# Seven stores of a pair of feed-forward chunks, placed over two units instead of one

## The chip, the cores and the metric

The kernel runs on one core of a Trainium2 chip. A core has five engines with an instruction queue each: TensorE (PE in the profile, with its weight loads as PEld) multiplies matrices, VectorE (DVE) and ScalarE (ACT) work on tiles, GpSimd (POOL) does so more slowly, and SyncE (SP) only issues DMA transfers here. An engine takes its instructions in the order of its queue; engines wait for each other at semaphores. SBUF is the on-chip memory, PSUM the banks into which TensorE accumulates, and DRAM the memory outside the core.

The metric is the device time of one execution in microseconds, the median of the runs. The kernel before takes 2773.14 us (three runs, 2771.61 to 2774.72).

## The reference, cut to what matters

Two layers of a decoder, 1024 tokens by 1024 features, all in float32. The change is in the feed-forward half of a layer:

```python
    h2 = rmsnorm(x, norm2[l])
    up = h2 @ w_up[l]
    a, v = up[..., :D_FF], up[..., D_FF:]
    a = causal_depthwise_conv(a, conv_w[l], conv_b[l])
    x = x + (jax.nn.gelu(a, approximate=False) * v) @ w_down[l]
```

`D_FF` is 2816, so `w_up` is 1024 x 5632 and `w_down` is 2816 x 1024; the convolution looks at the present token and the two before it.

## The kernel before, in words

**Numbers in two halves.** A float32 operand goes to TensorE as a rounded part (`hi`, made by a copy on ScalarE) and the rest (`lo`, a subtraction on VectorE). `split` (L122 to L124) issues the two. Every product is then three matmuls: hi by hi, hi by lo, lo by hi.

**Seven products for eight.** Most large products are two by two block products with seven block multiplications in place of eight. That needs sums and differences of blocks: of the weights, of the activations, and of the results.

**The up projection.** The 2816 hidden features are 22 chunks `j` of 128 features. Chunks 0 and 1 are done plainly (`up_plain`, L1353). Chunks 2 to 21 are units of `up(j)` (L1394): seven products w1, w5, w6, w3, w7, w2, w4 in this order, each 12 matmuls of 128x512 through `seven` (L851), with a `yield` in the middle and one after, so that a unit has 14 steps. The results gather in PSUM banks `pa` (`u_a`), `pc` (`u_c`) and `pb` (`u_b`). Bank `pa` takes w1, then w6 on top, then w7, then w4; before each further product an engine reads what is there. L1422 and L1430 are copies on ScalarE after w1 and w6. L1439, on VectorE, adds `pa` after w7 to `u5`; then w4 is accumulated on top and read in the gating. L1435 and L1444 are the like sums of `pc` and `pb`.

While unit j runs, the weights of unit j+1 are loaded (L1400, tag `ql`, two buffers), summed (L1404, L1405 and L1414 on GpSimd, L1409 on VectorE) and split (`piece`, L845). The words `"turn"` in unit j say when that goes on by one part: after w6 come L1404 and L1405, after L1435 the split of the next w1, after L1439 comes L1409 and the split of w5, after L1444 the split of w6.

In the second half of the last product the convolution of the chunk begins (L1252 on ScalarE, L1254 and L1255 on VectorE); GELU (L1257) follows at step 2 of the next unit and the gating (`gated`, L1276: L1280 twice on VectorE, one for each half of the tokens) at step 3.

**What is handed to the down projection.** The down projection (`down`, L1458) again uses seven products, over pairs of chunks, an even j and the odd j+1. With the two token halves of the even chunk called c11 and c12, and of the odd chunk c21 and c22 (`C[j-1]` and `C[j]`), it needs seven operands for each pair, numbered 0 to 6. Some are the halves themselves and four are differences, made on GpSimd by `less` (L1284). `spill(j, i, src)` (L1309) puts one operand out: a buffer `g` of tag `p4` (four buffers, which the odd chunks' products `cv` also use, and in the down projection weights of the groups after the first), a split into it (one ScalarE copy, one VectorE subtraction, shown in the profile at L123 and L124 as `g<-cv`), and a DMA of 512 KB to DRAM (L1313, `gd<-g`, in SP's queue). The even chunk's products are in one buffer (tag `ot`; for chunk 0 in one of the two `ql` buffers).

**Order.** `at(k, f)` (L1231) puts `f` down for k steps after the present one, and `chain` (L1315) runs what is due after each step's matmuls are issued. In the stage of the units 2 to 21 (L1612) the order on TensorE, ScalarE, VectorE and GpSimd is the order in which the program issues its instructions; elsewhere only TensorE's is, and a scheduler orders the others by priority when the program is built. SP's queue is ordered by that scheduler everywhere.

Of the kernel before, what the change touches and what calls it, by code (L numbers as in the profile page):

```python
# [11 lines left out]
ALU = mybir.AluOpType  # L12
# [9 lines left out]
NF = DFF // P  # L22
# [24 lines left out]
def f32(ap):  # L47
    return ap.bitcast(F32)
# [3 lines left out]
def trunk_kernel(ctx, tc, x, norm1, w_in, b_gate, w_br, w_o, norm2, w_up, conv_w, conv_b, w_down, norm_f, out, depth=None, probe=None):  # L52
    nc = tc.nc
    act, dve, pe, pool = nc.scalar, nc.vector, nc.tensor, nc.gpsimd
# [67 lines left out]
    def split(hi, lo, src):  # L122
        act.copy(hi, src)  # L123
        dve.tensor_tensor(lo, src, f32(hi), ALU.subtract)  # L124
# [1100 lines left out]
    def ffn(l, pending, final):  # L1225
# [3 lines left out]
        C, due, now = {}, {}, [0, 0]  # L1229

        def at(ahead, f):  # L1231

            due.setdefault(now[0] + ahead, []).append(f)
# [42 lines left out]
        def gated(j, n, v):  # L1276


            c = C[j][n]
            dve.tensor_tensor(c, c, v, ALU.mult)  # L1280
            C[j, n] = True
            both = (j, 1 - n) in C

            def less(dst, a):  # L1284

                return lambda: pool.tensor_tensor(dst, a, dst, ALU.subtract)  # L1286

            if j % 2 == 0:
                c11, c12 = C[j]
                if n == 0:  # L1290
                    at(2, lambda: spill(j, 0, c11))
                if both:
                    at(3, less(c11, c12))
                    at(5, lambda: spill(j, 5, c11))
            else:
                s1, c12 = C[j - 1]
                if n == 1:
                    at(1, less(c12, c))
                    at(1, less(s1, c))
                    at(2, lambda: spill(j, 6, c))  # L1300
                    at(3, lambda: spill(j, 2, c12))
                    at(4, lambda: spill(j, 1, s1))
                if both:
                    c21 = C[j][0]
                    at(5, less(s1, c21))
                    at(5, lambda: spill(j, 4, c21))
                    at(7, lambda: spill(j, 3, s1))

        def spill(j, i, src):  # L1309

            g = sb.tile([P, 2, HF], F32R, tag="p4", bufs=4, name="g")
            split(g[:, 0, :], g[:, 1, :], src)
            nc.sync.dma_start(gd[j // 2, i], f32(g))  # L1313
# [26 lines left out]
        def part(j, vv, n, w, halo):  # L1340
            o = bank("s" if vv else "ps", "u_ps")
            yield from product(o, [(w[k], h_part(n, k)) for k in range(KD)])
            with tc.high_priority(offset=AHEAD):
                if vv == 0:
                    conv_half(j, n, o, halo)
                else:
                    gated(j, n, o)
            yield
# [23 lines left out]
        def sums():  # L1372

            new_s(1)
            new_s(2)
            for i in range(4):
                b11, b12, b21, b22 = B[1, i], B[0, i], B[1, 4 + i], B[0, 4 + i]
                dve.tensor_tensor(b11, b12, b11, ALU.subtract)
                split(*S[1][i], b11)
                yield  # L1380
                dve.tensor_tensor(b12, b22, b11, ALU.subtract)
                split(*S[2][i], b12)
                yield
                dve.tensor_tensor(b22, b21, b12, ALU.subtract)
                yield
# [8 lines left out]
        def up(j):  # L1394
# [57 lines left out]
            next(cv)  # L1452
            at(3, lambda: next(cv))
            at(4, lambda: (gated(j, 0, u5), gated(j, 1, pa)))
            yield

# [145 lines left out]
        both = sums()  # L1602
# [190 lines left out]
```

## Time and profile before

| | |
|---|---|
| median of three runs | 2773.14 us |
| the profiled execution | 2774.87 us, of it a span of 2773.1 us |
| TensorE busy | 2679.4 us, 97% |
| VectorE, ScalarE, GpSimd busy | 72%, 49%, 25% |
| up projection of layer 0, layer 1 (units 2 to 21) | about 774 to 1170 us, 2145 to 2544 us |
| stores to the down projection | 154 in all, 7 for each of 11 pairs in 2 layers |

Rows in order of time read: start, duration, engine, line and operation, output and input, and in brackets how long the engine was idle before it and what ended that. Rows of neighbours of one kind are merged, with their count. Rows of waits read: who waited, for whom, the total in us, how many times, the longest. Times are microseconds from the start of the span. An operation's recorded duration overlaps its successor's a little, so VectorE's 128x512 operations are recorded with 0.68 us and follow each other every 0.60 us. The label of a releaser is the last event seen before the wait ended, which need not be the one that was waited for. Rows of stretches (from:to) give the length, then for PE, PEld, DVE, ACT and POOL the busy time and the number of instructions, then the granted TensorE clock, the DMA share and GB/s.

### The profile page before, as it was taken

To read this page: it belongs to the slowest core of one execution; us is meant where nothing else is said; L and a number is where in the kernel's file an instruction comes from. 1 tells how busy PE (TensorE), PEld (TensorE's weight loads), DVE (VectorE), ACT (ScalarE), POOL (GpSimd) and SP (SyncE) were. 2 spreads that over 40 slices of the span, in tenths; PEclk is the share of its full clock that TensorE was granted. 3 is DMA by queue.
4 is the path that set the end of the run, shared out by engine and by line. 5 is a ranking of instruction groups with operands and counts; after the bars stand their busy time and mean duration, and the time that the engine had idled before them with its cause. 6 is when DMAs were issued, how large, how long until landed. Compare 5 with 4: busy or idle time off the path is not lost. (4 is left out here: it accounts for less than half of the span.)

```text
span 2773.1 us, 36571 instructions
## 1 busy us (share of the span) xinstructions
PE 2679.4 (97%) x13066; PEld 2237.9 (81%) x13066; DVE 1989.5 (72%) x2952; ACT 1354.6 (49%) x2494; POOL 691.9 (25%) x485
## 2 busy tenths in 40 slices
PE   8999999989999999999999999999799999999999
PEld 8878888878877777788888788888687778777888
DVE  5877656564878888896657775565658788888865
ACT  5656545464544554422345555455544445454225
POOL 1005121232243433331210041121311333343200
PEclk9999999999999999999999999999899999999999
DMA  5012278663234444688411122885732443446863
GB/s 152 25 46 80 65 198 244 201 230 111 81 120 154 157 147 144 222 320 294 148 34 39 35 89 84 227 243 177 227 88 73 152 152 130 167 140 248 327 234 122
DMA packets 362305, 424.77 MB, mean 153 GB/s; under 512 B 25244, under 2 KB 289804, under 8 KB 360588
## 3 DMA queue, kind: packets, MB, share of 16 engines
q1 hardware_dynamic: 362124, 422.44, 46.2%
q8 instruction: 103, 1.69, 0.3%
q14 instruction: 78, 0.64, 0.1%
HBM read 282.78 MB, written 139.59 MB: 152 GB/s over the span
## 5 line engine op out<-in xcount | busy, mean ns | idle before, releaser
L124 DVE TENSOR_TENSOR w_lo<-up_a,w_hi 128x512 fp32r<-128x512 f32 x240 | 231.7, 966 | 37.9 <-ACT w_hi L123 37.9
L123 ACT CAST w_hi<-up_a 128x512 fp32r<-128x512 f32 x240 | 149.4, 622 | 172.4 <-PE u_b L855 38.3
L1549 DVE TENSOR_TENSOR x<-x,d_ps 128x512 f32<-128x512 f32 (+1 forms) x228 | 152.2, 671 | 81.5 <-PE d_ps L1543 80.5
L1286 POOL TENSOR_TENSOR cv<-cv 128x512 f32<-128x512 f32 x88 | 126.0, 1444 | 266.4 <-DVE g L124 130.4
L124 DVE TENSOR_TENSOR g<-cv,g 128x512 fp32r<-128x512 f32 x154 | 168.2, 1102 | 0.1
L124 DVE TENSOR_TENSOR w_lo<-w_raw,w_hi 128x512 fp32r<-128x512 f32 x152 | 116.1, 769 | 67.0 <-ACT w_hi L123 63.5
L123 ACT CAST w_hi<-w_raw 128x512 fp32r<-128x512 f32 x152 | 93.9, 620 | 119.4 <-PE o_ps L150 66.3
L124 DVE TENSOR_TENSOR w_lo<-in_a,w_hi 128x512 fp32r<-128x512 f32 x120 | 90.6, 755 | 83.2 <-ACT w_hi L123 83.0
L854 PE MATMUL u_a<-hh,w_hi 128*128 128x512 f32 x320 | 127.2, 398 | 19.3 <-ACT g L123 15.6
L123 ACT CAST w_hi<-in_a 128x512 fp32r<-128x512 f32 x120 | 74.5, 621 | 132.9 <-PE i_c L855 52.3
L1541 PE MATMUL d_ps<-gd_in,w_hi 128*128 128x512 f32 (+1 forms) x340 | 130.7, 384 | 6.3 <-ACT g L123 5.8
L123 ACT CAST g<-cv 128x512 fp32r<-128x512 f32 x154 | 93.6, 620 | 77.1 <-DVE g L124 41.4
L1542 PE MATMUL d_ps<-gd_in,w_hi 128*128 128x512 f32 (+1 forms) x340 | 130.5, 384 | 0.0
L1543 PE MATMUL d_ps<-gd_in,w_lo 128*128 128x512 f32 (+1 forms) x340 | 130.3, 383 | 0.0
L856 PE MATMUL u_a<-hh,w_lo 128*128 128x512 f32 x320 | 125.9, 393 | 4.5 <-DVE w_lo L124 4.5
L855 PE MATMUL u_a<-hl,w_hi 128*128 128x512 f32 x320 | 125.6, 393 | 0.0
L854 PE MATMUL u_a<-t_hi,w_hi 128*128 128x512 f32 x320 | 124.6, 389 | 0.4 <-ACT u L1422 0.4
L856 PE MATMUL u_a<-t_hi,w_lo 128*128 128x512 f32 x320 | 124.5, 389 | 0.0
L855 PE MATMUL u_a<-t_lo,w_hi 128*128 128x512 f32 x320 | 124.5, 389 | 0.0
L614 DVE TENSOR_TENSOR_SCAN stay<-stay,zero 128x128 f32<-128x128 f32 (+3 forms) x64 | 86.8, 1357 | 38.8 <-ACT stay L612 38.6
L1541 PE MATMUL d_ps<-gd_in,wd 128*128 128x512 f32 (+1 forms) x292 | 113.9, 390 | 0.0
L1543 PE MATMUL d_ps<-gd_in,wd 128*128 128x512 f32 (+1 forms) x292 | 112.8, 386 | 0.0
(397 smaller groups left out, 8617.2 us busy)
## 6 DMA issues: line engine op xcount, KB each, us to landing
gd<-g SPq DMA_DIRECT2D x154, 512.0 KB, 3.1
gd_in<-gd SPq DMA_DIRECT2D x154, 512.0 KB, 5.9
up_a<-in_w_up_dram SPq DMA_DIRECT2D x80, 512.0 KB, 4.6
t_kq<-tk SPq DMA_DIRECT2D x32, 768.0 KB, 5.8
wd_raw<-in_w_down_dram SPq DMA_DIRECT2D x22, 1024.0 KB, 8.2
w_raw<-in_w_in_dram SPq DMA_DIRECT2D x80, 256.0 KB, 3.3
in_a<-in_w_in_dram SPq DMA_DIRECT2D x40, 512.0 KB, 5.7
gin<-gs SPq DMA_DIRECT2D x32, 512.0 KB, 4.6
```

Source lines behind the costliest of these rows:

```text
L123: act.copy(hi, src)
L124: dve.tensor_tensor(lo, src, f32(hi), ALU.subtract)
L614: dve.tensor_tensor_scan(rev, rev, zero[:, 0:1].to_broadcast([P, L]), 1.0, ALU.mult, ALU.add)
L854: pe.matmul(o, w[0][:, c], rh, start=(first and i == 0), stop=False, skip_group_check=True)
L855: pe.matmul(o, w[0][:, c], rl, start=False, stop=False, skip_group_check=True)
L856: pe.matmul(o, w[1][:, c], rh, start=False, stop=(last and i == 3), skip_group_check=True)
L1286: return lambda: pool.tensor_tensor(dst, a, dst, ALU.subtract)
L1541: pe.matmul(o[:, sub], wh[:, c], gh[:, sub], start=(i == 0 and k in (0, 4, 5)), stop=False, skip_group_check=True)
L1542: pe.matmul(o[:, sub], wh[:, c], gl[:, sub], start=False, stop=False, skip_group_check=True)
L1543: pe.matmul(o[:, sub], wl[:, c], gh[:, sub], start=False, stop=(i == m - 1), skip_group_check=True)
L1549: dve.tensor_tensor(x, x, o[:, sub], ALU.add)
```

## The change

Only `gated` changes. In steps after the gating of the chunk, the seven stores and the differences stand as follows:

| | before | after |
|---|---|---|
| even chunk: store 0, difference, store 5 | 2, 3, 5 | 3, 4, 6 |
| odd chunk: first two differences | 1 | 1 |
| odd chunk: stores 6, 2, 1, 4, 3 | 2, 3, 4, 5, 7 | 1, 4, 7, 11, 14 |
| the same for chunk 1 | 2, 3, 4, 5, 7 | 2, 3, 4, 5, 7 |
| the same for chunk 21 | 2, 3, 4, 5, 7 | 8, 11, 14, 17, 20 |
| third difference (c21 less s1) | 5 | with store 2 |
| where the third difference is put | over s1 | into c22's place (`c`) |

A unit has 14 steps, so after the change store 3 of a pair falls on step 3 of the next odd unit, ahead of that step's gating. The number of stores, splits, transfers and differences is the same.

```diff
-            C[j, n] = True
-            both = (j, 1 - n) in C
-
-            def less(dst, a):
-
-                return lambda: pool.tensor_tensor(dst, a, dst, ALU.subtract)
+
+            later = (2, 3, 4, 5, 7) if j == 1 else (8, 11, 14, 17, 20) if j == NF - 1 else (1, 4, 7, 11, 14)
+
+            def less(dst, a, b):
+                return lambda: pool.tensor_tensor(dst, a, b, ALU.subtract)
 
             if j % 2 == 0:
                 c11, c12 = C[j]
                 if n == 0:
-                    at(2, lambda: spill(j, 0, c11))
-                if both:
-                    at(3, less(c11, c12))
-                    at(5, lambda: spill(j, 5, c11))
-            else:
+                    at(3, lambda: spill(j, 0, c11))
+                else:
+                    at(4, less(c11, c12, c11))
+                    at(6, lambda: spill(j, 5, c11))
+            elif n == 1:
                 s1, c12 = C[j - 1]
-                if n == 1:
-                    at(1, less(c12, c))
-                    at(1, less(s1, c))
-                    at(2, lambda: spill(j, 6, c))
-                    at(3, lambda: spill(j, 2, c12))
-                    at(4, lambda: spill(j, 1, s1))
-                if both:
-                    c21 = C[j][0]
-                    at(5, less(s1, c21))
-                    at(5, lambda: spill(j, 4, c21))
-                    at(7, lambda: spill(j, 3, s1))
+                c21 = C[j][0]
+                at(1, less(c12, c, c12))
+                at(1, less(s1, c, s1))
+                at(later[0], lambda: spill(j, 6, c))
+                at(later[1], lambda: spill(j, 2, c12))
+
+                at(later[1], less(c, c21, s1))
+                at(later[2], lambda: spill(j, 1, s1))
+                at(later[3], lambda: spill(j, 4, c21))
+                at(later[4], lambda: spill(j, 3, c))
```

## The prediction

> **What bounds the kernel now.** I read the page first, then the waits in total, then TensorE's rows in order of time, then the other engines' rows beside one wait.
>
> ```profile
> span 2773.1 us, 36571 instructions
> PE 2679.4 (97%) x13066; PEld 2237.9 (81%) x13066; DVE 1989.5 (72%) x2952; ACT 1354.6 (49%) x2494; POOL 691.9 (25%) x485
> ...
> PE u_a L854 <- ACT g L123: 15.6, 18, 0.9
> ACT g L123 <- DMA gd<-g: 25.1, 18, 2.2
> ```
>
> TensorE is busy for 97% of the span, so only a stall of TensorE is worth time. One stall of the up projection comes 18 times, about 0.87 us each, and is put down to a conversion `g` of a store. In order of time:
>
> ```profile
> 834.76 0.47 PE L854 MATMUL u_a<-hh,w_hi 128*128 128x512 f32 x1 [0.87 <-ACT g L123]
> ...
> 1013.50 0.39 PE L854 MATMUL u_a<-hh,w_hi 128*128 128x512 f32 x1
> ...
> 1027.10 0.39 PE L854 MATMUL u_b<-hh,w_hi 128*128 128x512 f32 x1
> ...
> 1030.85 0.47 PE L854 MATMUL u_a<-hh,w_hi 128*128 128x512 f32 x1 [0.87 <-ACT g L123]
> ...
> 1049.98 0.39 PE L854 MATMUL u_a<-hh,w_hi 128*128 128x512 f32 x1
> ...
> 1148.46 0.47 PE L854 MATMUL u_a<-hh,w_hi 128*128 128x512 f32 x1 [0.86 <-ACT g L123]
> ```
>
> An even unit starts at 1013.50; its sixth product (w2, `u_b`) starts at 1027.10, so a product of 12 matmuls takes 13.60/5 = 2.72 us. The seventh (w4, `u_a`) was due 2.72 later, at 1029.82, and starts at 1030.85: 1.03 us late. (From here on, times within this pair of units are written without their first two digits, 29.82 for 1029.82.) The stall returns at 834.76, 1148.46 and seven times between, every 313.70/8 = 39.21 us; two units of seven products need 14 x 2.72 = 38.08. **Each pair of chunks loses 1.13 us** (1.03 and a slow first matmul). There are 9 such pairs in each of 2 layers. The odd unit does not stall: its w4 starts at 49.98.
>
> The label names the event that came last. The w4 product accumulates into the bank that L1439 has just read into `u5`, so the operation it must wait for is VectorE's L1439. VectorE's rows from the even unit:
>
> ```profile
> 1020.28 1.56 DVE L124 TENSOR_TENSOR w_lo<-up_a,w_hi 128x512 fp32r<-128x512 f32 x1 [0.47 <-ACT w_hi L123]
> 1021.76 1.80 DVE L124 TENSOR_TENSOR g<-cv,g 128x512 fp32r<-128x512 f32 x1
> 1023.48 1.78 DVE L124 TENSOR_TENSOR w_lo<-up_a,w_hi 128x512 fp32r<-128x512 f32 x1
> 1025.19 2.38 DVE L124 TENSOR_TENSOR g<-cv,g 128x512 fp32r<-128x512 f32 x2
> 1027.49 0.67 DVE L1435 TENSOR_TENSOR u<-u,u_c 128x512 f32<-128x512 f32 x1
> 1028.09 1.42 DVE L124 TENSOR_TENSOR w_lo<-up_a,w_hi 128x512 fp32r<-128x512 f32 x1
> 1029.43 0.68 DVE L124 TENSOR_TENSOR g<-cv,g 128x512 fp32r<-128x512 f32 x1
> 1030.03 0.67 DVE L1439 TENSOR_TENSOR u<-u,u_a 128x512 f32<-128x512 f32 x1
> 1030.63 0.68 DVE L1409 TENSOR_TENSOR up_a<-up_a 128x512 f32<-128x512 f32 x1
> ```
>
> VectorE has no gap here. L1439's operand was ready when w7 ended, at 27.10; it runs at 30.03 to 30.70, and TensorE goes on 0.15 later. Four `g` of the odd chunk's stores stand ahead of it. Some operations take 0.68, others 1.4 to 1.8; GpSimd's rows say why:
>
> ```profile
> 1019.98 3.03 POOL L1286 TENSOR_TENSOR cv<-cv 128x512 f32<-128x512 f32 x2 [6.34 <-DVE cv L1280]
> 1022.97 1.75 POOL L1404 TENSOR_TENSOR up_s<-up_a 128x512 f32<-128x512 f32 x1
> 1024.80 1.62 POOL L1405 TENSOR_TENSOR up_a<-up_a 128x512 f32<-128x512 f32 x1
> 1027.65 1.31 POOL L1286 TENSOR_TENSOR cv<-cv 128x512 f32<-128x512 f32 x1 [1.23 <-DVE g L124]
> ```
>
> The two engines take turns. L1404 ends at 24.72 and the `w_lo` begun at 23.48 ends at 25.26, 0.54 later; L1405 then ends at 26.42, 1.16 after that. The last L1286 ends at 28.96, the `w_lo` of 28.09 at 29.51. But L1435, which reads one operand from PSUM, overlaps that L1286 at its usual 0.67. The Trainium skill says this too (SBUF — State Buffer, "Who interferes with whom"): VectorE with two SBUF inputs and GpSimd exclude each other for a whole instruction, whoever starts first, while VectorE with one SBUF input does not contend. By this rule the trace agrees; it speaks against the change as far as a sum is moved forward to where VectorE is short, and if L1435 contended as well, the walk below would end 1.16 later and about 0.7 of the stall would be left.
>
> **The change part by part.**
>
> *Ten even units to a layer, nine of them steady: stores spread.* Up to the second `g` (started 25.19) nothing moves: store 6 goes from step 2 to 1 and store 2 from 3 to 4 after gating, and between those steps only matmuls stand. Store 1 moves from step 4 to 7, store 4 from 5 to 11; both pass behind L1439, two `g` of 0.60 pitch (30.03 - 29.43). The third difference (in before it waited 1.23 for `g` to have read s1, because it overwrote s1) now goes to the free half c and starts behind L1405. The walk, from these rows: the second `g` ends 26.42 + 0.54 = 26.96; the difference ends 26.96 + 1.16 = 28.12; L1435 runs 26.88 to 27.55, untouched; `w_lo` of w1 waits and ends 28.12 + 0.54 = 28.66; L1439 runs 28.58 to 29.25; TensorE could go on at 29.40, due is 29.82. **The stall goes, with 0.42 to spare**: 18 x 1.13 = 20.3 us. ScalarE's conversion of w1 was there early enough:
>
> ```profile
> 1024.35 0.62 ACT L123 CAST w_hi<-up_a 128x512 fp32r<-128x512 f32 x1 [0.35 <-PE u_c L855]
> 1030.19 0.62 ACT L123 CAST g<-cv 128x512 fp32r<-128x512 f32 x1 [2.46 <-DVE g L124]
> ```
>
> Were that `g` of 30.19 what TensorE waits for, it too would be gone from this place.
>
> *Where the work goes.* Store 1 runs behind L1409 and w5, store 4 after the convolution of the even unit, store 3 at step 3 of the odd unit, ahead of its gating; stores 0 and 5 of the even chunk and their difference slip one step. Nothing is added: the same 7 stores (7 ScalarE, 7 VectorE, 7 DMAs) and 4 differences to a pair. In the odd unit:
>
> ```profile
> 1047.46 0.69 DVE L1439 TENSOR_TENSOR u<-u,u_a 128x512 f32<-128x512 f32 x1 [0.83 <-PE u_a L856]
> ```
>
> VectorE was idle for 0.83 before it, and 48.15 + 0.15 is 1.68 before w4 starts at 49.98. Cover is 2.5 us; one `g` is 0.6, and 1.16 more if it meets GpSimd: 1.8. I cost it at nothing; without cover it would be 0.6 to 1.8 a pair. Queued behind that `g` on ScalarE are the copy of `u5` and w2's conversion, and TensorE needs those one and three products (2.7 and 8.2 us) after the end of w5, which the copy waits for.
>
> *First pair (other steps, 2,3,4,5,7).* Its stores keep their steps; only the third difference moves, from step 5 to 3, and frees s1.
>
> ```profile
> 784.61 1.28 DVE L124 TENSOR_TENSOR g<-cv,g 128x512 fp32r<-128x512 f32 x2
> 788.11 0.68 DVE L124 TENSOR_TENSOR w_lo<-up_a,w_hi 128x512 fp32r<-128x512 f32 x1
> 794.13 0.69 DVE L124 TENSOR_TENSOR w_lo<-up_a,w_hi 128x512 fp32r<-128x512 f32 x1 [4.14 <-ACT w_hi L123]
> 794.74 0.68 DVE L1439 TENSOR_TENSOR u<-u,u_a 128x512 f32<-128x512 f32 x1
> ...
> 788.85 1.26 SPq L1400 DMA_DIRECT2D up_a<-in_w_up_dram  x2
> ...
> 795.57 0.47 PE L854 MATMUL u_a<-hh,w_hi 128*128 128x512 f32 x1 [1.12 <-DVE u L1439]
> ...
> 2166.37 0.68 DVE L1439 TENSOR_TENSOR u<-u,u_a 128x512 f32<-128x512 f32 x1
> ...
> 2167.19 0.77 PE L854 MATMUL u_a<-hh,w_hi 128*128 128x512 f32 x1 [2.51 <-DVE u L1439]
> ...
> 2167.20:2172.00 4.80, 4.80 (x14) 3.87 (x15) 2.45 (x4) 1.72 (x3) 2.23 (x2) 0.65 0.78 203
> ```
>
> Here L1439 stands behind a `w_lo` whose weights were loaded late: the load is issued at 788.85, when w4's `w_lo` frees one of two `ql` buffers. The other one holds chunk 0's products (s1 lives there) and in before is free only after store 3. In after its last reader is store 1's `g`: 785.89, or 787.0 once the earlier difference holds it up by 1.16. The load is issued 1.85 earlier, if the queue's order, fixed when the program is built, lets it: L1439 ends at 793.6, TensorE could go on at 793.7 and was due at 795.57 - 1.12 - 0.16 = 794.29. That is 1.3 + 0.1. In the second layer the same 1.85 leaves 0.8 of 2.67; and there 14 matmuls took 4.80 at a clock of 0.65 instead of 14 x 2.72/12 = 3.17, so 1.6 more comes back: 3.5. Bounds for both together: 0 and 5.7; I take 4.8, as the buffer is what the load waits for. The Trainium skill (TensorE: Matmul & The Clock Gate, Part 1) has the clock fall after an idle window of about 3.4 us; by it, no wait of 2.5 us would, and 1.6 would be left out of the sum. The row, with its 0.65, decides.
>
> *Last pair (8,11,14,17,20).* The down projection starts with a wait of 2.90 in both layers:
>
> ```profile
> 1178.07 0.68 DVE L1549 TENSOR_TENSOR x<-x,d_ps 128x512 f32<-128x512 f32 x1
> 1181.50 0.68 DVE L124 TENSOR_TENSOR g<-cv,g 128x512 fp32r<-128x512 f32 x1
> ...
> 1178.85 0.47 PE L1541 MATMUL d_ps<-gd_in,w_hi 128*128 128x512 f32 x1 [2.90 <-ACT g L123]
> ```
>
> The stores' `g` on VectorE come at 1181.50, after the stall, so moving them back does not shorten it: 0, with -6.1 (both waits gone) as one bound. The other: the odd product keeps its `p4` buffer longer, which weights of the next group want; one landing and one split late, some 4.5 us, twice: +9. I take 0. Chunk 0's shift by one step: 0, bounds one vector operation, 0.7, in each layer.
>
> ```profile
> gd<-g SPq DMA_DIRECT2D x154, 512.0 KB, 3.1
> ```
>
> **Sum.** 20.3 + 4.8 = 25.1. The profiled execution took 2774.87 us (span 2773.1 and 1.8 around it): 2749.8. The runs' median, 2773.14, lies 1.7 lower, so I expect a median of **2748**. Own range 2743 (a down wait gone, both clock drops spared) to 2755 (no gain in the first pair, a clock drop of 1.6 more).
>
> **The rivals.**
>
> *The pair of ports costs more.* The difference starts right behind L1405 and is let in before the second `g`, or L1435 contends: 1.16 on top of the walk, L1439 ends at 30.41, w4 starts 0.74 late, and 0.84 of 1.13 stays. At half that (a hold is shared, as in the `w_lo` of 28.09 with 0.74) 0.3 stays. Gain 5 to 15, and the first pair. For it: GpSimd comes three times in a row. Against: the row of L1435. About 2757.
>
> *The time is given back in the odd unit.* Store 3, gating and w2 meet L1404, L1405 and the difference, each held 1.16: 3.5 + 0.6 against 2.5 of cover, a stall of 1.6 in place of 1.13: 2773 + 18 x 0.5 - 4.8 = 2777. Against: in before two of the three already meet VectorE.
>
> *Slower: stores caught in the queue.* Loads and stores share SP's queue in order. If the stores of steps 11 and 14 stand behind a weight load that waits for w4 of the odd unit (in the even unit that `w_lo` ends at 25.26, 11.8 after the start), four `p4` buffers are taken: the product pair and three stores. ScalarE then waits at a `g` as it did for 25.1 us in 18 cases, with w2 behind it; 11.8 + 3.1 landing + 2 for conversion and difference is 17 against 13.6 where w2 is due: 3.4 a pair, 18 x (3.4 - 1.13) = +41, about 2814. It decides only once all four are held at step 3. Against: I count three, and the product pair comes free there.
>
> **How the numbers follow.** Forecast 0.60, ports 0.24, a down wait gone as well (2742) 0.03, given back 0.07, slower 0.06. A run of this kernel tells 0.2%, 5.5 us, from no change. Faster is 0.87, same 0.07, slower 0.06. The range is 2743 to 2761.
>
> **What would show it.** In the even units no wait at L854 on `u_a`, starts of equal products 38.08 apart, L1439 ending near 29.25 on this clock, the third difference right behind L1405; the load after the first pair issued some 2 us earlier. Wrong would be: a wait at u_a that stays over 0.3, a new wait in odd units, ScalarE waiting for `gd<-g`, or a longer start of the down projection.

## The result, and the profile after

The kernel after takes 2749.09 us (median of four runs, 2747.96 to 2751.60), the kernel before on the same chip 2773.93 (four runs): a ratio of 0.9913, with a 95% interval of 0.9900 to 0.9925. The profiled execution took 2748.3 us, with a span of 2746.1 against 2773.1, 27.0 us less.

In what follows the lines of the kernel after are named by their new numbers: L1437 is L1439 of before (the sum `u5`), L1433 is L1435, L1403 is L1405, L1398 is L1400, L1539 is L1541, L1547 is L1549, L1285 is L1286, L1311 is L1313, L1407 is L1409, L1420 is L1422. Edits shift the numbers a little further: the sum `u5` is L1438 and L1441 in two of the edited kernels.

The page of after, its first two rows:

```profile
span 2746.1 us, 36499 instructions
...
PE 2669.7 (97%) x13066; PEld 2235.0 (81%) x13066; DVE 1989.7 (72%) x2952; ACT 1351.9 (49%) x2494; POOL 687.1 (25%) x485
```

VectorE, ScalarE and GpSimd do what they did before to within 5 us; only when they do it has changed. The waits of TensorE in total, kernel after (who waited, for whom, total us, times, longest):

```profile
PE d_ps L1539 <- ACT g L123: 5.8, 2, 2.9
...
PE u_a L856 <- DVE w_lo L124: 4.2, 2, 2.1
...
PE u_a L854 <- DVE u L1437: 0.6, 2, 0.4
PE d_ps L1539 <- DVE x L1547: 0.3, 1, 0.3
```

The row of 18 waits of 0.87 us is gone, no wait of that size has come up in the up projections instead, and the first pair's two waits have gone from 3.6 to 0.6 us. The wait of 2.9 us at the start of each down projection stands as it was. TensorE's rows in order of time, kernel after:

```profile
779.33 0.50 PE L856 MATMUL u_a<-hh,w_lo 128*128 128x512 f32 x1 [2.10 <-DVE w_lo L124]
...
796.60 0.47 PE L854 MATMUL u_a<-hh,w_hi 128*128 128x512 f32 x1 [0.40 <-DVE u L1437]
...
1022.51 0.39 PE L854 MATMUL u_b<-hh,w_hi 128*128 128x512 f32 x1
...
1025.23 0.39 PE L854 MATMUL u_a<-hh,w_hi 128*128 128x512 f32 x1
...
1169.74 0.47 PE L1539 MATMUL d_ps<-gd_in,w_hi 128*128 128x512 f32 x1 [2.91 <-ACT g L123]
...
2136.56 0.50 PE L856 MATMUL u_a<-hh,w_lo 128*128 128x512 f32 x1 [2.11 <-DVE w_lo L124]
...
2153.61 0.47 PE L854 MATMUL u_a<-hh,w_hi 128*128 128x512 f32 x1 [0.19 <-DVE u L1437]
...
2526.68 0.47 PE L1539 MATMUL d_ps<-gd_in,w_hi 128*128 128x512 f32 x1 [2.91 <-ACT g L123]
```

The rows of before with the same work, where the prediction does not show them:

```profile
776.64 0.50 PE L856 MATMUL u_a<-hh,w_lo 128*128 128x512 f32 x1 [2.11 <-DVE w_lo L124]
...
2147.84 0.50 PE L856 MATMUL u_a<-hh,w_lo 128*128 128x512 f32 x1 [2.39 <-DVE w_lo L124]
...
2552.07 0.47 PE L1541 MATMUL d_ps<-gd_in,w_hi 128*128 128x512 f32 x1 [2.90 <-ACT g L123]
```

The seventh product of the even unit (w4) now starts 2.72 us after the sixth (1025.23 - 1022.51), on time. Laid beside each other, the two sets of rows say where the 27.0 us went; "shift" is after less before, and a part's share is the difference of two shifts:

| part | shift at its start | shift at its end | share |
|---|---|---|---|
| all that comes before the up projection of layer 0 | 0 | 779.33 - 776.64 = +2.69 | +2.69 |
| layer 0, first pair | +2.69 | 796.60 - 795.57 = +1.03 | -1.66 |
| layer 0, nine steady pairs | +1.03 | 1169.74 - 1178.85 = -9.11 | -10.14 |
| down of layer 0 up to the up projection of layer 1 | -9.11 | 2136.56 - 2147.84 = -11.28 | -2.17 |
| layer 1, first pair to w4 | -11.28 | 2153.61 - 2167.19 = -13.58 | -2.30 |
| layer 1, nine steady pairs | -13.58 | 2526.68 - 2552.07 = -25.39 | -11.81 |
| the rest | -25.39 | -27.0 | -1.6 |

Of the 27.0, 25.9 lie in the two up projections. The other rows hold the work of the other stages, with the last pair's stores in the down projections; they sum to -1.1, and single runs of the kernel after differ by 3.6. In these rows the granted clock differs between the two profiled executions: between 580 and 590 us, ahead of any edited work, it is 0.66 in before and 0.50 in after.

VectorE in the even unit, kernel after:

```profile
1020.59 1.78 DVE L124 TENSOR_TENSOR g<-cv,g 128x512 fp32r<-128x512 f32 x1
1022.29 0.67 DVE L1433 TENSOR_TENSOR u<-u,u_c 128x512 f32<-128x512 f32 x1
1022.89 1.18 DVE L124 TENSOR_TENSOR w_lo<-up_a,w_hi 128x512 fp32r<-128x512 f32 x1
1024.00 0.67 DVE L1437 TENSOR_TENSOR u<-u,u_a 128x512 f32<-128x512 f32 x1
```

GpSimd beside it:

```profile
1020.20 1.62 POOL L1403 TENSOR_TENSOR up_a<-up_a 128x512 f32<-128x512 f32 x1
1021.78 1.74 POOL L1285 TENSOR_TENSOR cv<-cv 128x512 f32<-128x512 f32 x1
```

Two `g` instead of four stand ahead of the sum `u5`. w2 starts at 1022.51 here and at 1027.10 in before, so 4.59 is added to compare with the walk of the prediction: the third difference ends at 23.52, that is 28.11 (28.12 in the walk); `u5` ends at 24.67, that is 29.26 (29.25). L1433 took its usual 0.67 while GpSimd was at work, as it did in before.

The odd unit, VectorE and then TensorE, kernel after:

```profile
1033.47 1.70 DVE L124 TENSOR_TENSOR g<-cv,g 128x512 fp32r<-128x512 f32 x1 [0.22 <-ACT g L123]
1035.10 1.78 DVE L1280 TENSOR_TENSOR cv<-cv,u 128x512 f32<-128x512 f32 x1
...
1041.94 0.68 DVE L1437 TENSOR_TENSOR u<-u,u_a 128x512 f32<-128x512 f32 x1
```

```profile
1041.55 0.39 PE L854 MATMUL u_b<-hh,w_hi 128*128 128x512 f32 x1
...
1044.27 0.39 PE L854 MATMUL u_a<-hh,w_hi 128*128 128x512 f32 x1
```

Store 3 (33.47) and the gating meet GpSimd and take 1.70 and 1.78. In before two other operations of this unit were held in the same way (1.78 at 1041.05 and 1.59 at 1043.16), in after there are three, with a split of 1.40 at 1039.80, so only one hold is new. VectorE no longer idles ahead of the sum, which ends at 42.62; with 0.15 it is 1.50 ahead of w4's start.

### The profile page after: what moved, and what is told of

The parts are those of the page before. It is cut to its first block, busy times and chain, and to the rows that moved or that the text cites. A ratio compares the mean times of both kernels' runs of the same rounds, so it can differ in the third digit from the quotient of the medians.

```text
span 2746.1 us, 36499 instructions
## 1 busy us (share of the span) xinstructions
PE 2669.7 (97%) x13066; PEld 2235.0 (81%) x13066; DVE 1989.7 (72%) x2952; ACT 1351.9 (49%) x2494; POOL 687.1 (25%) x485
## 4 chain that ended last, share of the span: by engine, by line
PE 47%; DVE 5%; DMA 1%; issue 1%; ACT 1%; POOL 1%; DVEq 0%; SPq 0%; ACTq 0%; POOLq 0%
PE d_ps L1539 4%; PE d_ps L1541 4%; PE d_ps L1540 4%; PE u_a L854 3%; PE u_a L856 3%; PE u_a L855 3%; PE u_c L856 1%; PE u_c L854 1%; PE u_c L855 1%; PE i_a L854 1%; PE i_a L855 1%; PE i_a L856 1%; PE o_ps L149 1%; PE o_ps L151 1%; PE o_ps L150 1%
## 5 line engine op out<-in xcount | busy, mean ns | idle before, releaser
L124 DVE TENSOR_TENSOR w_lo<-up_a,w_hi 128x512 fp32r<-128x512 f32 x240 | 223.6, 938 | 20.4 <-ACT w_hi L123 20.4
L1547 DVE TENSOR_TENSOR x<-x,d_ps 128x512 f32<-128x512 f32 (+1 forms) x228 | 152.3, 672 | 78.0 <-PE d_ps L1541 77.3
L1285 POOL TENSOR_TENSOR cv<-cv 128x512 f32<-128x512 f32 x88 | 132.6, 1518 | 276.8 <-DVE g L124 144.7
L1539 PE MATMUL d_ps<-gd_in,w_hi 128*128 128x512 f32 (+1 forms) x340 | 130.7, 384 | 6.1 <-ACT g L123 5.8
L1541 PE MATMUL d_ps<-gd_in,w_lo 128*128 128x512 f32 (+1 forms) x340 | 130.5, 384 | 0.0
L1539 PE MATMUL d_ps<-gd_in,wd 128*128 128x512 f32 (+1 forms) x292 | 113.9, 390 | 0.0
L1541 PE MATMUL d_ps<-gd_in,wd 128*128 128x512 f32 (+1 forms) x292 | 112.8, 386 | 0.0
L1540 PE MATMUL d_ps<-gd_in,wd 128*128 128x512 f32 (+1 forms) x292 | 112.8, 386 | 0.0
```

The lines of the kernel that those rows point to most:

```text
L1285: return lambda: pool.tensor_tensor(dst, a, b, ALU.subtract)
L1539: pe.matmul(o[:, sub], wh[:, c], gh[:, sub], start=(i == 0 and k in (0, 4, 5)), stop=False, skip_group_check=True)
L1540: pe.matmul(o[:, sub], wh[:, c], gl[:, sub], start=False, stop=False, skip_group_check=True)
L1541: pe.matmul(o[:, sub], wl[:, c], gh[:, sub], start=False, stop=(i == m - 1), skip_group_check=True)
L1547: dve.tensor_tensor(x, x, o[:, sub], ALU.add)
```

## The experiments

Each kernel was run beside the kernel before. The chips differ a little, so ratios are what is compared; 0.001 is 2.8 us. "Kernel after" or "kernel before" says which one is edited.

**Which operation does w4 wait for?** The label says ScalarE's `g`; the prediction says VectorE's L1439. One store is put two steps later in the kernel before, behind L1439, and nothing else:

```diff
-                    at(5, lambda: spill(j, 4, c21))
+                    at(7 if 1 < j < NF - 1 else 5, lambda: spill(j, 4, c21))
```

> The kernel before with one edit: in the steady pairs store 4 goes from step 5 to 7, so that its g stands behind L1439 on VectorE, while ScalarE still has a g at about the same place. Theory (TensorE waits for L1439): one VectorE operation of 0.60 us less ahead of it, the wait at u_a falls from 0.87 to about 0.27 in 18 pairs, 18 x 0.6 = 11 us: 2763 +- 2. Rival (TensorE waits for ScalarE's g, as the label of the wait says): wait unchanged at 0.87, 2774.

Measured 2766.08 us, ratio 0.9960 (0.9947 to 0.9974), 0.0040 or some 11 us less. A steady pair's wait on TensorE, then the sum on VectorE and the next `g` on ScalarE, kernel with this edit:

```profile
873.65 0.47 PE L854 MATMUL u_a<-hh,w_hi 128*128 128x512 f32 x1 [0.24 <-DVE u L1439]
...
872.83 0.67 DVE L1439 TENSOR_TENSOR u<-u,u_a 128x512 f32<-128x512 f32 x1
...
874.45 0.62 ACT L123 CAST g<-cv 128x512 fp32r<-128x512 f32 x1 [2.76 <-DMA gd<-g]
```

One VectorE subtraction of 0.60 pitch less ahead of L1439 takes 0.63 off each wait (0.87 to 0.24), 18 times 11.3; it is the same in all 18 pairs. The label is now L1439 itself. w4 starts 0.15 after the sum ends (873.50), and ScalarE's next `g` starts only at 874.45, when w4 is already running. So w4 waits for that sum; the `g` on ScalarE was only the last event seen.

**The new place of the third difference alone.** Kernel before, with the difference put into c at step 3 in every pair; all stores keep their steps (`less` takes its two operands apart from its output here, as in the kernel after):

```diff
+                    c21 = C[j][0]
+                    at(3, less(c, c21, s1))
                     at(4, lambda: spill(j, 1, s1))
-                if both:
-                    c21 = C[j][0]
-                    at(5, less(s1, c21))
                     at(5, lambda: spill(j, 4, c21))
-                    at(7, lambda: spill(j, 3, s1))
+                    at(7, lambda: spill(j, 3, c))
```

> The kernel before with one part of the change alone: in every pair the third difference goes to the free half c at step 3, all stores stay at steps 2, 3, 4, 5, 7. Theory (L1439 waits behind four g and three GpSimd sums; moving stores past it is what helps): the steady stall stays in all 18 pairs and grows, since the difference now holds the g of store 1 for 1.1 us where it held the w_lo of w1 for 0.74: 0.87 becomes about 1.2 us of wait, +0.4 x 18 = +7; the first pair gains about 5.5 (load issued about 1.8 us sooner). Together 2775 +- 3. Rival (the freed s1 and the earlier difference are what removes the steady stall): waits at u_a gone, about 2749.

Measured 2777.19 us, ratio 1.0001 (0.9992 to 1.0010). Two neighbouring steady waits, kernel with this edit:

```profile
832.30 0.47 PE L854 MATMUL u_a<-hh,w_hi 128*128 128x512 f32 x1 [1.20 <-ACT g L123]
...
871.86 0.47 PE L854 MATMUL u_a<-hh,w_hi 128*128 128x512 f32 x1 [1.20 <-DVE u L1438]
```

A pair now takes 39.56 us (871.86 - 832.30) instead of 39.21: 0.35 more, 18 times 6.3. That gives back what the first pair gains. Started behind L1405, the difference holds VectorE up while four `g` are still ahead of the sum. In the steady pairs the new place alone is a loss, as expected. And the same wait carries two labels in neighbouring pairs.

**The same, in the first pair only.** The edit above, for chunk 1 alone (`if j == 1`):

> The kernel before with the third difference moved to c and step 3 in the first pair of each layer alone. Theory (the earlier release of chunk 0's buffer lets the weight load go earlier): the load after the first pair is issued about 1.8 us sooner, the waits at u_a of 1.12 and 2.51 fall to 0.5 or less, the clock drop after the second goes: 5 to 5.5 us, 2768.5 +- 1.5; the 18 steady waits stay at 0.87. Rival (the load is hidden anyway, or the queue's order is not changed by it): 2774.

Measured 2772.37 us, ratio 0.9986 (0.9977 to 0.9995): 3.9 us less. The first pair's wait in layer 0, kernel with this edit:

```profile
795.71 0.47 PE L854 MATMUL u_a<-hh,w_hi 128*128 128x512 f32 x1 [0.30 <-DVE u L1441]
```

It was 1.12 in before, and in layer 1 no such wait is left; the 18 steady waits stay at 0.87. The gain is below the 5 to 5.5 us that were expected, though the interval (1.4 to 6.4 us) reaches them.

**Stores spread, the difference left over s1.** Kernel after, with store 3 put earlier so that the even chunk's one buffer is free in time for the next even chunk:

```diff
-            later = (2, 3, 4, 5, 7) if j == 1 else (8, 11, 14, 17, 20) if j == NF - 1 else (1, 4, 7, 11, 14)
+            later = (2, 3, 4, 5, 7) if j == 1 else (8, 11, 14, 17, 20) if j == NF - 1 else (1, 4, 7, 8, 9)
...
-                at(later[1], less(c, c21, s1))
                 at(later[2], lambda: spill(j, 1, s1))
+                at(5 if j == 1 else later[2], less(s1, c21, s1))
                 at(later[3], lambda: spill(j, 4, c21))
-                at(later[4], lambda: spill(j, 3, c))
+                at(later[4], lambda: spill(j, 3, s1))
```

> The changed kernel with the sum left over s1: stores of the steady pairs at 1, 4, 7, 8, 9, the difference behind store 1 (for chunk 1 at step 5 as before), so stores 1, 4 and 3 are past L1439 but within one unit. Theory: the steady stall is gone as in the changed kernel (18 x 1.13), with L1439 ending about 1.1 us sooner in its unit since the difference comes after it; only the first pair's gain of about 5.5 is missing: 2754 +- 2. Rival (the spread over two units is needed, three stores in the second half of the even unit stall it): a new wait before w3 or w7 of the odd unit, or at u_a, time between 2757 and 2774.

Measured 2756.23 us, ratio 0.9925 (0.9911 to 0.9938). The waits at w4, kernel with this edit:

```profile
PE u_a L854 <- DVE u L1437: 3.6, 2, 2.2
```

The steady waits are gone; the first pair's two are back at 3.6 us, as in before. So the steady gain comes from the stores alone, the first pair's from the difference alone, and the two add up: 0.0075 here and 0.0014 there, 0.0089 beside the 0.0087 of the kernel after. It also shows that the spread over two units is not what counts: all stores of these pairs are put out within nine steps of the gating, that is within the even unit, and the nine steady pairs of layer 0 take 373.2 us here as in the kernel after (373.1).

**How much margin is left?** Kernel after, with store 1 at step 5 instead of 7, ahead of the sum `u5` again:

```diff
-            later = ... else (1, 4, 7, 11, 14)
+            later = ... else (1, 4, 5, 11, 14)
```

> The kernel after, with store 1 of every steady odd chunk put out two steps earlier, so that its subtraction stands on VectorE ahead of the sum u5 (L1437) again; the other stores stay late. Theory (a walk with 0.42 us of margin): the sum ends 0.60 later, at 29.85 on the even unit's clock, TensorE could go on at 30.00 and was due at 29.82: late by 0.2 to 0.3 with the restart, 18 times, some +5 us against the kernel after, ratio 0.993 to the kernel before, and short rows of u_a waits of up to 0.2 us come back in the steady pairs. Rival (the margin is wider than one subtraction): no steady wait, no change, ratio 0.991. Second rival (a store is what TensorE waits for, wherever it stands): a wait of 0.5 us or more.

Measured 2753.08 us, ratio 0.9918 (0.9903 to 0.9933). TensorE and VectorE in the same even unit, kernel with this edit:

```profile
1024.15 0.39 PE L854 MATMUL u_b<-hh,w_hi 128*128 128x512 f32 x1
...
1027.05 0.47 PE L854 MATMUL u_a<-hh,w_hi 128*128 128x512 f32 x1
...
1027.82 0.40 PE L854 MATMUL u_a<-hh,w_hi 128*128 128x512 f32 x1
```

```profile
1025.62 0.68 DVE L124 TENSOR_TENSOR g<-cv,g 128x512 fp32r<-128x512 f32 x1
1026.23 0.67 DVE L1437 TENSOR_TENSOR u<-u,u_a 128x512 f32<-128x512 f32 x1
```

w4 was due at 24.15 + 2.72 = 26.87 and starts at 27.05: 0.18 late, the 30.00 less 29.82 of the walk; the fourth matmul of w4, three later, follows after 0.77 instead of 0.68, so a pair loses 0.27, 18 times 4.9. All 18 pairs show it: the nine of layer 0 take 375.64 us, 2.5 more than in the kernel after (373.14). The totals (+3 to +4 us) lie that way, though their intervals overlap; the rows decide. The margin of 0.42 us is real, and one subtraction more uses it up. The wait is too short for the list of waits, but the rows show it.

**The third difference three steps later.** Kernel after:

```diff
-                at(later[1], less(c, c21, s1))
+                at(later[2] if j > 1 else later[1], less(c, c21, s1))
```

> The kernel after, with the third difference of every steady pair on GpSimd put three steps later, from store 2 to store 1. Theory: it no longer holds up the split of w1 on VectorE by 1.16 us ahead of the sum u5, so that L1437 ends about 0.6 to 1.2 sooner in the even unit (28.1 to 28.7 on its clock instead of 29.26), but TensorE was on time already: time unchanged against the kernel after, ratio 0.991 with 0.002 to either side. Rival (the turns of VectorE and GpSimd still cost TensorE something in the steady pairs): 18 times up to 0.3, the time falls by up to 5 us, ratio 0.989 or less.

Measured 2748.92 us, ratio 0.9907 (0.9891 to 0.9924). GpSimd, kernel with this edit:

```profile
1019.66 1.62 POOL L1403 TENSOR_TENSOR up_a<-up_a 128x512 f32<-128x512 f32 x1
1021.24 1.75 POOL L1285 TENSOR_TENSOR cv<-cv 128x512 f32<-128x512 f32 x1
```

The difference did not move: it still follows L1403 at once. GpSimd has no other instruction between steps 4 and 7, so its queue is the same, and a step only sets a place in a queue, not a time. The edit says nothing of the theory; it is one more measurement of the kernel after.

**The kernel after once more**, unchanged, on the chip of the three that follow:

> The changed kernel itself, beside the next three on the same chip: 2749 by every theory, no wait at u_a in steady pairs, waits of 2.91 at the start of the down projection.

Measured 2752.56 us, ratio 0.9911 (0.9897 to 0.9925).

**The last pair.** Kernel after, with the last pair's stores at (1, 4, 7, 11, 14) as in the others:

```diff
-            later = ... else (8, 11, 14, 17, 20) if j == NF - 1 else ...
+            later = ... else (1, 4, 7, 11, 14) if j == NF - 1 else ...
```

> The changed kernel with the stores of the last pair at steps 1, 4, 7, 11, 14 in place of 8, 11, 14, 17, 20. Theory (the later steps do not shorten the start of the down projection and hold a p4 buffer that the weights wad wait for): the waits of 2.91 stay, ScalarE's waits for gd<-g at the weights get shorter, the wait of 0.3 at 1200 of layer 0 goes; 0 to -0.5 us against the changed kernel. Rival (the later steps keep VectorE free at the start of the down projection): waits there longer than 2.91, +1 to +5 us.

Measured 2751.47 us, ratio 0.9906 (0.9892 to 0.9920): no difference that can be told. The two waits at the start of the down projection stay at 2.9, the one of 0.3 at 1200.47 is gone as expected, and one of 1.6 for a weight's copy (`wd`) has come up. The late stores neither shorten nor lengthen the wait of 2.9 at the start.

**What is that wait of 2.9?** The next product in the first result bank of the down projection must wait for VectorE's add that reads that bank (`x<-x,d_ps`). By the order of instructions in the built program it stands fourth among the adds of its step in after, behind those of three other banks: at the seam between the stage in program order and the scheduled one, three adds are still put down in order and the first one is left to the scheduler. If that is the cause, ending the ordered stage one step earlier removes the wait. Kernel after, in `chain`:

```diff
                 now[1] = i
+                if i == NF:
+                    yield
                 then = units[i + 1] if i + 1 < len(units) else iter(())
```

> The changed kernel with one more edit: the stage in which the program's order is the engines' order ends before the first step of the down projection, not after it. In the changed kernel the add of the first quarter (L1547, first bank) stands fourth on VectorE, behind the adds of the second, third and fourth. Theory (the wait of 2.91 is for that add, which was put behind nine other VectorE operations): the wait falls to about 1.2 us, where the second weight's lo becomes what is late; 2 x 1.8 and a clock drop less in some runs, 2745 +- 2. Rival (the wait is for ScalarE's g, as labelled, or for the weights): still 2.9, 2749.

Measured 2745.41 us, ratio 0.9884 (0.9870 to 0.9898). VectorE, kernel after, the first and the last of the four adds; the last ends at 1169.63, just ahead of TensorE's start at 1169.74:

```profile
1164.15 0.69 DVE L1547 TENSOR_TENSOR x<-x,d_ps 128x512 f32<-128x512 f32 x1
...
1168.95 0.68 DVE L1547 TENSOR_TENSOR x<-x,d_ps 128x512 f32<-128x512 f32 x1
```

TensorE, kernel with this edit:

```profile
1166.61 0.40 PE L1542 MATMUL d_ps<-gd_in,w_hi 128*128 128x512 f32 x1
1167.88 0.50 PE L1543 MATMUL d_ps<-gd_in,w_lo 128*128 128x512 f32 x1 [0.88 <-DVE w_lo L124]
```

The two waits of 2.91 are gone and two of 0.9, for a weight's split, are left: 4.0 us less, and 0.3 for the wait at 1200.47 shown below. The adds now come in the order of the banks, but the edit also changes the places of a weight's split and of the convolution among them, so the add is not moved quite alone. The total fell by 0.0027, some 7 us, 3 more than the waits explain; the intervals of the two ratios just meet (0.9898 and 0.9897). The profiled executions show where such an excess can come from: in the kernel after on the same chip both waits of 2.91 are followed by a stretch at a lower clock (0.62 from 1168.0 to 1172.5, 0.72 from 2529.0 to 2535.0), here the clock stays at 1.00 in both places. Whether it is so in every run stays open. By its ratio it is the fastest kernel of the study, ahead of both before and after.

**One step further.** That kernel, with the GELU and gating of chunk 21 five steps later, to give the weight's split VectorE's time:

```diff
-            at(3, lambda: next(cv))
-            at(4, lambda: (gated(j, 0, u5), gated(j, 1, pa)))
+            late = 5 if j == NF - 1 else 0
+            at(3 + late, lambda: next(cv))
+            at(4 + late, lambda: (gated(j, 0, u5), gated(j, 1, pa)))
```

> The kernel of e9 with GELU and gating of chunk 21 five steps later. Theory: two VectorE operations of 0.60 leave the space ahead of the second weight's lo, so that the wait at the start of the down projection falls by another 0.6 to 1.2 us in each layer: 2743 +- 2. Rival (the scheduler already lets the weights go first): same as e9.

Measured 2746.65 us, ratio 0.9889 (0.9875 to 0.9903). A miss: the wait stays, 0.89 ahead of the matmul at 1166.64. VectorE works without a gap there, and the operations ahead of that split are the same, in the same order, in both kernels: one half's gating still stands ahead of it, the other stood behind it already. So the edit took nothing out of its way, which is nearer to the rival than to the theory.

## Why the prediction was right, point by point

**The stall and its cause.** That w4 waits for VectorE's sum and not for the `g` of the label was an inference from the rows; moving one store past the sum shows it (0.63 off each wait).

**18 x 1.13 = 20.3.** Layer 0's nine pairs measured 10.14, that is 1.127 each. Layer 1's measured 11.81, which is 10.2 and the 1.6 of the clock drop that the prediction counted with the first pair: where the first pair alone was edited, that drop is missing and the 18 waits are not, and the same nine pairs take 383.25 us (2549.90 - 2166.65) against 384.88 in before. The stretch behind w4 there, kernel after:

```profile
2153.00:2158.00 5.00, 4.81 (x22) 3.68 (x20) 2.45 (x5) 1.25 (x3) 2.57 (x2) 1.00 1.05 364
```

The clock is 1.00, where it was 0.65 in before, and 5.00 us hold 22 matmuls of 0.227.

**The walk.** It gave the ends of the third difference and of the sum to 0.01 us. The rival in which the turns of VectorE and GpSimd cost more falls: L1433 was not held, and the second `g` came first (1020.59 to 1022.37, with the difference in behind it until 1023.52). The Trainium skill (SBUF — State Buffer, "Who interferes with whom") has VectorE instructions with one SBUF input free of GpSimd; the 0.67 of L1433 beside the 1.74 of L1285 agrees. The experiment on the margin shows that the margin of 0.42 was no accident of the walk: 0.60 more ahead of the sum makes w4 0.18 late.

**The odd unit at nothing.** Store 3 met GpSimd, at 1.70, as the prediction allowed (up to 1.8), and the gating behind it as well, at 1.78. The sum still ends 1.50 before it is needed, against 1.68 in before. The rival that gives the time back there falls.

**Stores caught in the queue.** ScalarE's waits for a `g` buffer, kernel after:

```profile
ACT g L123 <- DMA gd<-g: 1.2, 2, 0.7
```

In before they were 25.1 us in 18 cases; the two that are left lie in the down projection, where weights' copies now wait for stores as well (below). The rival that ends slower falls.

**The first pair, 1.4 + 3.5, taken as 4.8.** It measured 1.66 and 2.30 + 1.6 = 3.9, so 5.6 for 4.8. The mechanism held, and a part of the excess is luck with the clock. SyncE's queue, kernel after:

```profile
786.84 2.63 SPq L1311 DMA_DIRECT2D gd<-g  x2
789.78 1.26 SPq L1398 DMA_DIRECT2D up_a<-in_w_up_dram  x2
```

The load was issued at 788.85 in before, which is 791.54 with the shift of 2.69: 1.76 earlier, for 1.85 in the prediction. A wait of 0.40 stayed in layer 0 where the prediction had none, because in before a stretch at a lower clock lies in this pair and made w4 due later. Stretches from the start to the end of the pair's products, before and then after (the clock is the third number from the right):

```profile
776.60:795.50 18.90, 17.81 (x70) 14.23 (x70) 12.49 (x16) 7.88 (x15) 5.91 (x4) 0.91 0.56 191
```

```profile
779.30:796.60 17.30, 16.50 (x71) 13.01 (x71) 12.51 (x16) 7.78 (x15) 5.87 (x4) 1.00 0.47 148
```

TensorE needed 17.81 us of work there in before and 16.50 in after. The due time came forward too, so nearly the whole of the load's lead became time, and the wait did not vanish. The other run of the kernel after settles it, since the stretch at a lower clock is there as in before:

```profile
777.80:795.60 17.80, 17.77 (x71) 14.24 (x71) 12.48 (x16) 7.77 (x15) 6.14 (x5) 0.90 0.49 157
```

The products of the pair begin at 777.83 there and w4 at 795.59. So w4 is late by less than 0.2, near the none that was forecast, and the pair takes 17.76 us against 18.93 in before: 1.17 for the 1.4 of the prediction. So some 0.5 of the 1.66 came from the clock. In layer 1 the sum came 2.31 earlier (2166.37 less the shift of 11.28, against 2152.78), more than the load's 1.85; why it gained more was not followed.

**The last pair at nothing.** The wait of 2.91 stayed in both layers, as forecast from the stores' place behind it. The loss that the prediction bounded, stores that hold their `p4` buffers longer, did occur once, small. ScalarE and then TensorE, kernel after, in layer 0:

```profile
1198.48 0.62 ACT L123 CAST wd<-wd_raw 128x512 fp32r<-128x512 f32 x1 [4.68 <-DMA gd<-g]
```

```profile
1200.47 0.50 PE L1539 MATMUL d_ps<-gd_in,w_hi 128*128 128x512 f32 x1 [0.32 <-DVE x L1547]
```

A weight's copy into a `p4` buffer waits for a store to land (12.9 us in 5 cases in all), and TensorE waits 0.32 for what queues behind it; without the late stores this wait is gone (another of 1.6 came up, and the total did not tell the two apart).

**The sum.** 20.3 + 5.6 = 25.9 beside the predicted 25.1, about 0.5 of it the clock in the first pair; what lies outside the up projections adds 1.1 in the profiled execution. The median fell by 24.8. That it lies within 0.3 of the 25.1 is closer than the runs can tell, since single runs of the kernel after differ by 3.6.

## What to carry to other kernels

Where an accumulating engine waits for a bank to be read, count what stands ahead of the reader in its engine's queue, and move out of that queue's way whatever has no due time of its own; here it was enough to get it past the reader, and further spreading bought nothing. Walk the moved rows one after the other with their held durations before trusting a margin, since here 0.6 us, one instruction, lay between no stall and 18. And look at seams between two ways of ordering a program: there one add came fourth that should have come first, and the edit that put it first took 4.0 us off two waits, more than a tenth of the whole change.

## What the runs showed that was not expected

**A label can flip.** With the third difference alone in its new place, the same wait of 1.20 us is put down to ScalarE's `g` at 832.30 and to VectorE's sum at 871.86, one pair later in one run. What is waited for is read from the engine's rows, not from the label.

**The same wait is followed by a lower clock in one place and not in another.** The kernel after, the first 3.5 us behind the same wait of 2.91 in layer 0 and in layer 1:

```profile
1169.70:1173.20 3.50, 3.46 (x9) 2.79 (x10) 3.50 (x4) 1.25 (x2) 2.20 (x3) 0.58 0.48 194
...
2526.60:2530.10 3.50, 3.42 (x15) 2.88 (x16) 3.50 (x4) 1.25 (x2) 2.25 (x2) 1.00 0.26 105
```

The program is the same at both places, and the wait too; after the one TensorE gets 9 matmuls through, after the other 15. In before it was the other way round:

```profile
1178.80:1182.80 4.00, 3.95 (x17) 3.30 (x18) 4.00 (x5) 1.24 (x2) 2.23 (x2) 1.00 0.39 158
...
2552.00:2556.00 4.00, 3.93 (x11) 3.15 (x12) 4.00 (x5) 1.24 (x2) 2.24 (x2) 0.61 0.43 174
```

The Trainium skill (TensorE: Matmul & The Clock Gate, Part 1) describes a window of about 3.4 us that runs free of the program, so that it matters where in the window an event falls; these rows do not contradict it, but no run here shows the window itself. It also has the clock fall after an idle window of that length; here waits of 2.5 us (before, at 2167.19) and 2.9 us were followed by a lower clock in some cases. In the second pair of rows 17 matmuls pass in the one stretch and 11 in the other, 6 x 0.227 = 1.4 us lost in these 4 us alone. Single runs of the kernel after scatter by 3.6 us (2747.96 to 2751.60), and what lies ahead of the up projection of layer 0 moved by 2.7 between the two profiled executions, with a lower clock from 580 to 590 us in after; two such stretches more or less would be enough for it, though no run here shows that they are the cause.
